# The value side of a head on the other head's partitions, in a kernel for an RG-LRU and RWKV-7 trunk

## The chip, the core and the metric

One core of one Trainium2 chip runs the whole layer as one program. The metric is the device time of one execution in microseconds; lower is better. The time before is 2658.46 us, the median of three runs (2656.79 to 2659.37).

## What is computed

One layer over 512 tokens of width 2048: a projection of the normed input, two token mixers beside each other (an RG-LRU on 1024 channels, RWKV-7 on 16 heads of 64 channels), an output projection, a gated FFN with a short causal convolution, a gated embedding and a last norm. The change touches RWKV-7. Cut to it, the reference is:

```python
def wkv7_scan(r, decay, k, v, kk, kka):
    def step(state, inp):
        r_t, w_t, k_t, v_t, kk_t, b_t = inp
        sa = jnp.einsum('bhvk,bhk->bhv', state, -kk_t)
        state = (state * w_t[:, :, None, :] + sa[..., None] * b_t[:, :, None, :]
                 + v_t[..., None] * k_t[:, :, None, :])
        y = jnp.einsum('bhvk,bhk->bhv', state, r_t)
        return state, y
...
        y = wkv7_scan(rh.astype(jnp.float32), heads(decay), kh.astype(jnp.float32),
                      vh.astype(jnp.float32), kk, kk * ah)
        mean = jnp.mean(y, axis=-1, keepdims=True)
        var = jnp.mean(jnp.square(y - mean), axis=-1, keepdims=True)
        yn = ((y - mean) * lax.rsqrt(var + LNX_EPS)).reshape(B, S, D_RWKV).astype(x.dtype)
        yn = yn * rwkv_lnx_w[i] + rwkv_lnx_b[i]
        bonus = (jnp.sum(rh * kh * rwkv_rk[i], axis=-1, keepdims=True) * vh).reshape(B, S, D_RWKV)
        out_b = (yn + bonus) * g
        h = h + jnp.concatenate([out_a, out_b], axis=-1) @ w_o[i]
```

Each head keeps a 64x64 state that is decayed, corrected and added to at every token.

## The kernel before, in words

**Dense products.** Every large product is made of three: each operand is split into a high and a low part (`split`, `wfill_`), and `dense` (lines 157, 159, 161) multiplies high by high, low by high and high by low, each a product of 128 rows, 128 columns and 512 moving columns. The weights come by DMA into `wraw`, and ScalarE and VectorE make `whi` (line 127) and `wlo` (line 128) of them.

**Phase 1** does the projection, both mixers and the first part of the output projection; **phase 2** the rest of the output projection, the FFN and what follows (lines 1170 and on). The change lies in phase 1, in the steps for the RWKV heads.

**Head pairs.** Two heads of 64 channels share a tile of 128 partitions: head half 0 on partitions 0 to 63, half 1 on 64 to 127. There are eight such pairs (`NP`). The 512 tokens are cut into eight chunks of 64 (`NC`, `C`). For each pair:

- `prep` makes, from the projections `kt`, `rt`, `vt`, the decayed operands: `bt` and `ktl` (lines 698 to 705), `AR` (709, 710), the gate `gt` and the bonus `bv`, and `pcs`, the decay of each whole chunk.
- `batch` does what needs no state, for all eight chunks. `scores` (764 to 771) multiplies `bt` and `ktl` by `AR`, chunk by chunk and half by half (64 rows, 64 columns, 128 moving columns), and VectorE masks the results into `MQ` and `NQ`. `prod` (808 to 813) makes products of 32x32 tiles, four quarters at a time, which double the size of a triangular inverse from 2 to 32; line 849 and line 862 close it to 64, `TT`. `turn` (782 to 791) transposes an operand (ScalarE copies, VectorE transposes 32x32 blocks) into `vk`, `ak`, `bk`, `kk2`. `each` (774 to 779) makes 16 products of 64 rows, 64 columns and 64 moving columns, one per chunk and half, and ScalarE copies the result out: `X1` from `NQ` and `vk`, `WT` from `ak` and `TT`, and `X1` again from `TT` and `X1`.
- `chain` (874 to 923) carries the state `st` through the chunks: `us` from `st` (lines 891, 893), the new state from `kk2` times `vk` (897) plus `bk` times `us` (906), scaled by the chunk's decay and added to the decayed old state `so` (912 to 914), and the output `y` from `vk` times `NQ` (899), `st` times `AR` (902) and `us` times `MQ` (917). All of these are 64x64x64 products, one per half.
- `norm` (926 to 943) normalizes `y`, adds the bonus and gates.

Every one of the 64-row products of before works on one half: its operands lie on the 64 partitions of that half, and so do its results. The products are full float32 (not split); in the trace each leaves two records.

**What sets the order.** On TensorE the order is that of the code (`manual_schedule`). `merge` (359 to 423) interleaves the generators: the dense stream yields after each product, and `prep`, `chain`, `batch` and `norm` yield the time on TensorE that their step is thought to take and the delay until the next step. The delays are the table `W` (line 17): `t0`, `tg`, `tt` for the batch, `lu`, `ls` for the chain, `dpace` the least distance. `duo` (732 to 747) runs the chain of one pair and the batch of the next in lockstep: a round is one step of each, back to back, followed by dense products. The chain has 15 steps, the batch 12. VectorE, ScalarE, GpSimd and SyncE are ordered by a scheduler that goes by the priorities set with `high_priority`; each engine then works strictly in that order.

**Buffers.** The results of small products go to three PSUM buffers `wk` (`aux`), two `ch` and one `y`; those of the dense stream to two `mm`.

Of the kernel before, what the change touches and what calls it, by code (L numbers as in the profile page):

```python
# [52 lines left out]
def shape_constants():  # L53
# [21 lines left out]
    c[:, o:o + 128] = (p[:, None] // 64 == p[None, :] // 64) / 64.0  # L75
# [10 lines left out]
class Builder:  # L86
# [441 lines left out]
    def lora_z(self):  # L528
# [29 lines left out]
        for tt in range(4):  # L558
            z = self.t(k1, ("vk", "bk", "kk2", "vk")[tt], (128, LW), bufs=2)
            SC.activation(z, ps[tt][:, 0:LW], AF.Copy)  # L560
            self.zl.append(z)
# [188 lines left out]
    def batch(self, j, q):  # L750
# [13 lines left out]
        def scores(src, dst, half):  # L764
            ps = wk()
            for i in range(4):
                c = 4 * half + i
                for hs in H2:
                    TE.matmul(ps[hs, i * 128:(i + 1) * 128].rearrange("p (a t) -> p a t", a=2), src[hs, c * C:(c + 1) * C],
                              AR[hs, :, c, :], start=True, stop=True)  # L770
            V.tensor_tensor(dst[:, half * 4:half * 4 + 4, :], ps.rearrange("p (i t) -> p i t", t=128), m3, ALU.mult)


        def each(lhs, rhs, dst):
            ps = wk()
            for c in range(NC):
                for hs in H2:
                    TE.matmul(ps[hs, c * C:(c + 1) * C], lhs(hs, c), rhs(hs, c), start=True, stop=True)
            SC.activation(dst, c3(ps), AF.Copy)


        def turn(n, src, bufs):
            d_ = T(n, bufs, (128, NC, C))
            SC.activation(fl(d_), src, AF.Copy)
            s3 = c3(src)
            for h in range(2):
                for i in range(2):
                    a_, b_ = 64 * h + 32 * i, 64 * h + 32 * (1 - i)
# [4 lines left out]
        for half in range(2):  # L793
            scores(bt, MQ, half)
# [21 lines left out]
        for b in (2, 4, 8, 16):  # L816
# [6 lines left out]
            if b == 2:  # L823
                scores(ktl, NQ, 0)
            with self.tc.high_priority(offset=W['offt'] - self.OFFS):
                if b == 2:

                    vk = turn("vk", vt, 2)
# [7 lines left out]
                if b == 16:  # L836
                    kk2 = turn("kk2", ktl, 2)
# [4 lines left out]
            if b == 2:  # L842
                scores(ktl, NQ, 1)
# [12 lines left out]
        X1 = NQ[:, :, 0:64]  # L856
# [733 lines left out]
```

## Time and profile before

| | |
|---|---|
| median of three runs | 2658.46 us (2656.79 to 2659.37) |
| the profiled execution | 2656.44 us, of which its span 2654.6 us |
| TensorE products busy | 2631.0 us |
| VectorE busy | 1698.6 us |
| ScalarE busy | 1089.4 us |
| stretch 70 to 850 us (the eight head pairs) | TensorE 773.90 of 780.00 us, VectorE 487.16, ScalarE 395.09 |

The span goes from the first to the last instruction of one execution; the profiled execution's own time is 1.8 us longer. In the profile PE stands for TensorE's products, PEld for its weight loads, DVE for VectorE, ACT for ScalarE, POOL for GpSimd, SP for SyncE. A row of the timeline gives the start in us, the length in us, the engine, the line, the operation, what is written and what it is made from (without buffer numbers), the shape, and how many records it merges; in brackets stands the idle time before it. Ends of products are modelled, so the distance between starts is what they cost in a stream. A row of the groups gives the count after x, then busy time, the mean length of one in ns, and idle time before with what ended it.

### The profile page before, as it was taken

The numbers are of one execution on the slowest core, as the hardware profiler recorded it, in microseconds if no ns is written. First come the engines' busy times: TensorE is split into PE (matmuls) and PEld (weight loads), VectorE is DVE, ScalarE is ACT, GpSimd is POOL, SyncE is SP. The second block draws the span as 40 slices with busy tenths as digits, with TensorE's granted clock in tenths as the row PEclk, the third lists the DMA queues.
The fourth block names the chain that finished last, engine by engine and source line by source line (L and its number), as shares of the span: only waits on it lengthen the run. The fifth ranks groups of instructions, "written<-read, shape, count | busy, mean of one in ns | idle before, by whom it ended". The sixth has DMA issues, their size and how long they took to land.

```text
span 2654.6 us, 43517 instructions
## 1 busy us (share of the span) xinstructions
PE 2631.0 (99%) x18434; PEld 2164.0 (82%) x18434; DVE 1698.6 (64%) x2356; ACT 1089.4 (41%) x1554; POOL 218.9 (8%) x177
## 2 busy tenths in 40 slices
PE   9999999999999999999999999999999999999997
PEld 8877777787777888888888888888888888888887
DVE  5764676477655635667676766766666667775447
ACT  6474546446533433333333333333333333335335
POOL 0010101001111300000000000000000000000000
PEclk9999999999999999999999999999999999999999
DMA  7222222222333322232232323233232323332223
GB/s 250 90 77 69 81 77 73 69 84 78 100 124 117 115 88 95 98 109 97 99 106 95 103 96 103 97 102 104 98 109 97 110 96 103 104 107 85 99 92 108
DMA packets 84483, 265.56 MB, mean 100 GB/s; under 512 B 9792, under 2 KB 12480, under 8 KB 84288
## 3 DMA queue, kind: packets, MB, share of 16 engines
q1 hardware_dynamic: 84288, 262.78, 30.0%
q8 instruction: 144, 2.36, 0.4%
q14 instruction: 51, 0.42, 0.1%
HBM read 254.62 MB, written 8.13 MB: 99 GB/s over the span
## 4 chain that ended last, share of the span: by engine, by line
PE 86%; DVE 3%; ACT 2%; issue 1%; POOL 1%; DMA 0%; POOLq 0%; DVEq 0%; ACTq 0%
PE wk L1212 12%; PE wk L1213 12%; PE wk L1211 12%; PE mm L1294 6%; PE mm L1295 6%; PE mm L1293 6%; PE mm L161 5%; PE mm L159 5%; PE mm L157 5%; PE mm L1384 2%; PE mm L1386 2%; PE mm L1385 2%; PE wk L812 1%; PE mm L1211 1%; PE mm L1213 1%
## 5 line engine op out<-in xcount | busy, mean ns | idle before, releaser
L127 ACT ACTIVATE whi<-wraw 128x1024 fp32r<-128x1024 f32 (+1 forms) x361 | 373.9, 1036 | 707.3 <-PE mm L159 173.5
L128 DVE TENSOR_TENSOR wlo<-wraw,whi 128x1024 fp32r<-128x1024 f32 (+1 forms) x361 | 440.7, 1221 | 210.6 <-ACT whi L127 205.6
L1211 PE MATMUL wk<-uh,whi 128*128 128x512 f32 x1408 | 547.8, 389 | 0.0
L1212 PE MATMUL wk<-ul,whi 128*128 128x512 f32 x1408 | 547.7, 389 | 0.0
L1213 PE MATMUL wk<-uh,wlo 128*128 128x512 f32 x1408 | 547.7, 389 | 0.0
L127 ACT ACTIVATE whi<-hw 128x1024 fp32r<-128x1024 f32 x154 | 163.3, 1060 | 464.6 <-PE wk L1212 418.6
L157 PE MATMUL mm<-xh,whi 128*128 128x512 f32 x832 | 329.6, 396 | 0.9 <-DVE hT L447 0.9
L161 PE MATMUL mm<-xh,wlo 128*128 128x512 f32 x832 | 330.4, 397 | 0.0
L159 PE MATMUL mm<-xl,whi 128*128 128x512 f32 x832 | 330.1, 397 | 0.0
L1211 PEld LDWEIGHTS wk<-uh,whi 128*128 128x128 f32 x1408 | 264.4, 188 | 54.8
L1213 PEld LDWEIGHTS wk<-uh,wlo 128*128 128x128 f32 x1408 | 264.3, 188 | 54.8
L1212 PEld LDWEIGHTS wk<-ul,whi 128*128 128x128 f32 x1408 | 264.4, 188 | 54.7
L128 DVE TENSOR_TENSOR wlo<-hw,whi 128x1024 fp32r<-128x1024 f32 x154 | 188.7, 1225 | 181.1 <-ACT whi L127 178.6
L1294 PE MATMUL mm<-wlo,hid 128*128 128x512 f32 x680 | 265.1, 390 | 0.0
L1295 PE MATMUL mm<-whi,hid 128*128 128x512 f32 x680 | 264.9, 390 | 0.0
L1293 PE MATMUL mm<-whi,hid 128*128 128x512 f32 x680 | 264.8, 389 | 0.0
L1239 POOL TENSOR_TENSOR tmp<-tmp,rsa 128x512 f32<-128x512 f32 x48 | 87.5, 1822 | 1360.9 <-ACT tmp L1238 1360.9
L157 PEld LDWEIGHTS mm<-xh,whi 128*128 128x128 f32 x832 | 156.3, 188 | 35.2 <-issue 2.1
L161 PEld LDWEIGHTS mm<-xh,wlo 128*128 128x128 f32 x832 | 156.2, 188 | 33.8 <-issue 1.9
L159 PEld LDWEIGHTS mm<-xl,whi 128*128 128x128 f32 x832 | 156.2, 188 | 33.7 <-issue 1.7
L1308 DVE TENSOR_TENSOR h<-h,mm 128x512 f32<-128x512 f32 x264 | 175.1, 681 | 0.6
L1293 PEld LDWEIGHTS mm<-whi,hid 128*128 128x128 f32 x680 | 127.7, 188 | 26.3
(521 smaller groups left out, 3581.7 us busy)
## 6 DMA issues: line engine op xcount, KB each, us to landing
wraw<-wgu SPq DMA_DIRECT2D x192, 512.0 KB, 3.2
hw<-wd SPq DMA_DIRECT2D x88, 512.0 KB, 3.2
wraw<-wz SPq DMA_DIRECT2D x80, 512.0 KB, 3.6
wraw<-wpg SPq DMA_DIRECT2D x31, 512.0 KB, 3.3
wraw<-wo SPq DMA_DIRECT2D x22, 512.0 KB, 3.4
wraw<-wo SPq DMA_DIRECT2D x20, 256.0 KB, 2.9
tmp<-xT SPq DMA_DIRECT2D x16, 256.0 KB, 2.7
wraw<-wd SPq DMA_DIRECT2D x8, 512.0 KB, 3.2
```

Of the source, the lines that this page charges most:

```text
L127: nc.scalar.activation(hi, raw, AF.Copy)
L128: nc.vector.tensor_tensor(lo, raw, hi.bitcast(F32), ALU.subtract)
L157: nc.tensor.matmul(ps, hi[:, k, :], xh, start=first and i == 0, stop=False)
L159: nc.tensor.matmul(ps, hi[:, k, :], xl, start=False, stop=False)
L161: nc.tensor.matmul(ps, lo[:, k, :], xh, start=False, stop=last and i == n - 1)
L1211: TE.matmul(ps, wh[:, k, :], xh, start=h + k == 0, stop=False)
L1212: TE.matmul(ps, wh[:, k, :], xl, start=False, stop=False)
L1213: TE.matmul(ps, wl[:, k, :], xh, start=False, stop=h == 1 and k == 7)
L1293: TE.matmul(ps, x[0][:, k, ts_], w[0][:, k, :], start=first and k == 0, stop=False)
L1294: TE.matmul(ps, x[0][:, k, ts_], w[1][:, k, :], start=False, stop=False)
L1295: TE.matmul(ps, x[1][:, k, ts_], w[0][:, k, :], start=False, stop=last and k == 1)
L1308: V.tensor_tensor(o, o, ps[tt], op)
```

## The change

The value channels of a head pair are stored with the two halves swapped: `prepare` swaps them in the weights of `vt`, in `mu_v`, in the gate's `rwkv_g2`, in the norm's gain and bias and in the rows of `w_o`; the constant `bdm` gets ones where the halves differ. So a value tile of half 0 lies on partitions 64 to 127. A product whose result is on the value side then takes its operands from the partitions of one half and writes to those of the other (`H2[1 - h]`, `H2[h ^ x]`), while products within the key side stay on their half as before. `scores` for `bt` (straight) and `ktl` (crossed) are made together, chunk by chunk. `each` takes several descriptions and issues their products next to each other: `X1` (crossed) with a new `Y0` (straight), `WT` (straight) with the product of `kk2` and `vk` (crossed).

The two sums that need no state leave the chunk loop: `Y0`, the part of the output from `vk` and `NQ`, is made in the batch and added to `y` at the end; the product of `kk2` and `vk`, scaled by `pcs`, is made in the batch into `kk2`, and the loop's `so` adds it to the decayed state, on VectorE instead of ScalarE. In the loop stay, per chunk, `us` and `st` times `AR`, then `bk` times `us` and `us` times `MQ`.

The batch yields once more, between the two halves of the scores (`t1`), and no longer makes scores between its 32x32 products. `vk` has one buffer instead of two. The table `W` has other numbers.

```diff
-W = dict(offw=10000, offp=[0, 300, 300, 100, 5000, 1000, 466], offl=100, offt=-100, pace=381, dpace=1914, late=16634, offs=3000, offd=300, start=1346, lora=5719, dec=0, rsk=8216, ready=23343, bonus=38816, t0=7550, tg=2186, tt=1559, lx=3928, lu=1429, ls=891, g1=1221753, g2=4936, g3=7972, per=[2, 3, 2, 2, 3, 1, 3, 0], dec7=2070)
+W = dict(offw=20000, offp=[0, 0, -100, -100, 5000, 1000, 5000], offl=0, offt=1000, pace=829, dpace=1914, late=16634, offs=45674, offd=20000, start=1496, lora=7732, dec=0, rsk=12832, ready=6791, bonus=38816, t1=891, t0=5837, tg=1544, tt=3247, lx=12605, lu=1133, ls=378, g1=2540239, g2=4936, g3=5800, per=[2, 3, 2, 3, 1, 2, 3, 0], dec7=1579)
...
-    c[:, o:o + 128] = (p[:, None] // 64 == p[None, :] // 64) / 64.0
+    c[:, o:o + 128] = (p[:, None] // 64 != p[None, :] // 64) / 64.0
...
-        def scores(src, dst, half):
-            ps = wk()
+        def scores(half):
+            pm_, pn = wk(), wk()
             for i in range(4):
                 c = 4 * half + i
-                for hs in H2:
-                    TE.matmul(ps[hs, i * 128:(i + 1) * 128].rearrange("p (a t) -> p a t", a=2), src[hs, c * C:(c + 1) * C],
-                              AR[hs, :, c, :], start=True, stop=True)
-            V.tensor_tensor(dst[:, half * 4:half * 4 + 4, :], ps.rearrange("p (i t) -> p i t", t=128), m3, ALU.mult)
+                for ps, src, x in ((pm_, bt, 0), (pn, ktl, 1)):
+                    for h in range(2):
+                        TE.matmul(ps[H2[h ^ x], i * 128:(i + 1) * 128].rearrange("p (a t) -> p a t", a=2), src[H2[h], c * C:(c + 1) * C],
+                                  AR[H2[h], :, c, :], start=True, stop=True)
+            for ps, dst in ((pm_, MQ), (pn, NQ)):
+                V.tensor_tensor(dst[:, half * 4:half * 4 + 4, :], ps.rearrange("p (i t) -> p i t", t=128), m3, ALU.mult)
-        def each(lhs, rhs, dst):
-            ps = wk()
+        def each(*what):
+            r = [c3(wk()) for _ in what]
             for c in range(NC):
-                for hs in H2:
-                    TE.matmul(ps[hs, c * C:(c + 1) * C], lhs(hs, c), rhs(hs, c), start=True, stop=True)
-            SC.activation(dst, c3(ps), AF.Copy)
+                for ps, (lhs, rhs, x) in zip(r, what):
+                    for h in range(2):
+                        TE.matmul(ps[H2[h ^ x], c, :], lhs[H2[h], c, :], rhs[H2[h], c, :], start=True, stop=True)
+            return r
...
-        for half in range(2):
-            scores(bt, MQ, half)
+        scores(0)
+        yield 960, W['t1']
+        scores(1)
...
-            if b == 2:
-                scores(ktl, NQ, 0)
...
-            if b == 2:
-                scores(ktl, NQ, 1)
...
-        each(lambda hs, c: NQ[hs, c, 0:64], lambda hs, c: vk[hs, c, :], X1)
+        for dst, ps in zip((X1, Y0), each((X1, vk, 1), (vk, Y0, 0))):
+            SC.activation(dst, ps, AF.Copy)
...
-        each(lambda hs, c: ak[hs, c, :], lambda hs, c: TT[hs, c, :], WT)
-        each(lambda hs, c: TT[hs, c, :], lambda hs, c: NQ[hs, c, 0:64], X1)
+        pw, pk = each((ak, TT, 0), (kk2, vk, 1))
+        SC.activation(WT, pw, AF.Copy)
+        V.tensor_tensor(kk2, pk, pcs.unsqueeze(2).broadcast_to([128, NC, C]), ALU.mult)
+        SC.activation(X1, each((TT, X1, 0))[0], AF.Copy)
...
             if c:
                 pu = ch()
                 for hs in H2:
                     TE.matmul(pu[hs, 0:64], MQ[hs, c, 0:64], st[hs], start=True, stop=True)
+                for h in range(2):
+                    TE.matmul(yo[H2[1 - h]], st[H2[h]], AR[H2[h], 1, c, :], start=True, stop=False)
                 us = T("us", 2, (128, 64))
                 V.tensor_tensor(us, pu[:, 0:64], NQ[:, c, 0:64], ALU.add)
-            if not last:
+                if c < NC - 1:
+                    so = T("so", 2, (128, 64))
+                    V.scalar_tensor_tensor(so, st, pc, kv[:, c, :], ALU.mult, ALU.add)
+                yield 350, W['lu']
+            if c < NC - 1:
                 ps = ch()
                 for hs in H2:
-                    TE.matmul(ps[hs, 0:64], kk2[hs, c, :], vk[hs, c, :], start=True, stop=False)
-            for hs in H2:
-                TE.matmul(yo[hs], vk[hs, c, :], NQ[hs, c, 64:128], start=True, stop=False)
...
+                    TE.matmul(ps[hs, 0:64], bk[hs, c, :], us[hs], start=True, stop=True)
+                st = T("st", 2, (128, 64))
+                V.scalar_tensor_tensor(st, ps[:, 0:64], pc, so, ALU.mult, ALU.add)
+            for h in range(2):
+                TE.matmul(yo[H2[1 - h]], us[H2[h]], MQ[H2[h], c, 64:128], start=c == 0, stop=True)
+            yield 250, W['ls']
...
-        SC.activation(sq, py, AF.Square)
-        SC.activation(y, py, AF.Copy)
+        V.tensor_tensor(y.rearrange("p (c t) -> p c t", t=C), py.rearrange("p (c t) -> p c t", t=C), NQ[:, :, 64:128], ALU.add)
+        SC.activation(sq, y, AF.Square)
...
+    def swap(a, axis=-1):
+        a = np.moveaxis(a, axis, -1)
+        return np.moveaxis(a.reshape(a.shape[:-1] + (NP, 2, 64))[..., ::-1, :].reshape(a.shape), -1, axis)
-        cols += [w[:, ZR + 1024:ZR + 2048][:, s], w[:, ZR:ZR + 1024][:, s], w[:, ZR + 2048:ZR + 3072][:, s]]
+        cols += [w[:, ZR + 1024:ZR + 2048][:, s], w[:, ZR:ZR + 1024][:, s], swap(w[:, ZR + 2048:ZR + 3072])[:, s]]
```

How the instructions move is shown at three places; x2 is one product per head half, x8 and x32 are merged likewise. The changed kernel's lines are numbered a little differently: 772 is the matmul of the scores, 822 that of `prod`, 902 and 904 are `us` and `st` times `AR`, 914 and 918 `bk` times `us` and `us` times `MQ`, 909 `so`, 916 `st`, 775 the mask.

First, TensorE in a round of a chain beside the 32x32 products of the next pair's batch, before:

```order
L161 MATMUL mm_4323<-xh_94_443,wlo_4250 128x512
L891 MATMUL ch_4498<-st_4438,MQ_3253 64x64 x2
L897 MATMUL ch_4503<-vk_3380,kk_543_3761 64x64 x2
L899 MATMUL y_4265<-NQ_3254,vk_3380 64x64 x2
L902 MATMUL y_4265<-AR_3063,st_4438 64x64 x2
L812 MATMUL wk_4510<-Tm_4299,MQ_4277 32x16 x32
L157 MATMUL mm_4323<-xh_97_461,whi_4249 128x512
```

The same kind of round on TensorE in the changed kernel:

```order
L157 MATMUL mm_5563<-xh_81_381,whi_5464 128x512
L902 MATMUL ch_5659<-st_5595,MQ_4357 64x64 x2
L904 MATMUL y_5477<-AR_4209,st_5595 64x64 x2
L822 MATMUL wk_5668<-Gm_5632,Tt_5546 32x16 x32
L159 MATMUL mm_5563<-xl_82_382,whi_5464 128x512
```

The products of `kk2` with `vk` and of `vk` with `NQ` are gone from the round, and the straight product L902 stands next to the crossed one, L904.

Second, TensorE at the start of the second head pair's batch, before:

```order
L897 MATMUL ch_2028<-vk_1306,kk_265_1638 64x64 x2
L899 MATMUL y_2027<-NQ_1186,vk_1306 64x64 x2
L906 MATMUL ch_2028<-NQ_1186,bk_1528 64x64 x2
L917 MATMUL y_2027<-MQ_1185,NQ_1186 64x64 x2
L769 MATMUL wk_2041<-AR_1870,bt_1811 64x128 x8
L769 MATMUL wk_2051<-AR_1870,bt_1811 64x128 x8
```

And now:

```order
L914 MATMUL ch_2088<-NQ_1187,bk_1537 64x64 x2
L918 MATMUL y_2087<-MQ_1186,NQ_1187 64x64 x2
L772 MATMUL wk_2097<-AR_1967,bt_1958 64x128 x2
L772 MATMUL wk_2098<-AR_1967,ktl_1963 64x128 x2
L772 MATMUL wk_2097<-AR_1967,bt_1958 64x128 x2
```

The scores from `bt` and from `ktl` alternate, chunk by chunk; before, those from `ktl` came a round later, behind the first 32x32 products.

Third, VectorE at the same head pair, where it makes `ktl`, before:

```order
L805 STREAM_TRANSPOSE Tm_2061<-Tt_2062 128x256
L703 TENSOR_TENSOR kt_1137<-kt_1137,ta_1661 128x512
L705 TENSOR_TENSOR ktl_1816<-kt_1137,th_1654 128x512
L981 TENSOR_TENSOR row_111<-mm_2005,rs_94 128x512
L893 TENSOR_TENSOR us_2129<-ch_2126,NQ_1186 128x64
```

And now:

```order
L128 TENSOR_TENSOR wlo_2076<-wraw_2073,whi_2075 128x1024
L916 SCALAR_TENSOR_TENSOR st_2091<-ch_2088,pcs,kk_268_1658 128x64
L703 TENSOR_TENSOR kt_1137<-kt_1137,ta_1684 128x512
L909 SCALAR_TENSOR_TENSOR so_2133<-st_2091,pcs,kk_268_1658 128x64
L705 TENSOR_TENSOR ktl_1963<-kt_1137,th_1677 128x512
L775 TENSOR_TENSOR MQ_2095<-wk_2097,con_175 128x512
```

`ktl` now stands behind the chain's first `st`, which reads what L914 above has made, and ahead of the first mask.

More of the change, by code (lines that the diff above doesn't have):

```diff
@@ L836, in batch @@
                 if b == 16:
-                    kk2 = turn("kk2", ktl, 2)
+                    kk2 = turn("kk2", ktl, 2, 1)
             yield 1100, W['tg']
@@ L886, in chain @@
             us = NQ[:, c, 0:64]
-            last = c == NC - 1
+            pc = pcs[:, c:c + 1]
+            so = kv[:, c, :]
             if c:
@@ L916, in chain @@
[L916 to L918 removed]
+                    TE.matmul(ps[hs, 0:64], bk[hs, c, :], us[hs], start=True, stop=True)
+                st = T("st", 2, (128, 64))
+                V.scalar_tensor_tensor(st, ps[:, 0:64], pc, so, ALU.mult, ALU.add)
+            for h in range(2):
+                TE.matmul(yo[H2[1 - h]], us[H2[h]], MQ[H2[h], c, 64:128], start=c == 0, stop=True)
+            yield 250, W['ls']
```

47 lines of the change are left out of this document (16 added, 31 removed).

## The prediction

> **What bounds the kernel now.** First the page, for which engine is full, then the busy time of the stage that the change touches.
>
> ```profile
> span 2654.6 us, 43517 instructions
> PE 2631.0 (99%) x18434; PEld 2164.0 (82%) x18434; DVE 1698.6 (64%) x2356; ACT 1089.4 (41%) x1554; POOL 218.9 (8%) x177
> PE 86%; DVE 3%; ACT 2%; issue 1%; POOL 1%; DMA 0%; POOLq 0%; DVEq 0%; ACTq 0%
> core 0: us, PE busy (x) PEld busy (x) DVE busy (x) ACT busy (x) POOL busy (x), PEclk, DMA share, GB/s
> 70.00:850.00 780.00, 773.90 (x9925) 616.01 (x9923) 487.16 (x838) 395.09 (x641) 92.22 (x79) 1.00 0.27 84
> ```
>
> TensorE (PE) is busy 99% of the span and carries 86% of the chain that ended last. In the stretch from 70 to 850 us, in which all eight head pairs run, it lacks 6.1 of 780 us; VectorE is busy 62% and ScalarE 51% of it. So time taken off PE's own stream there should come off the end, unless PE begins to wait. Its waits in that stretch are few:
>
> ```profile
> engine line waited for: us in total, times, longest us
> PE wk L769 <- DVE ktl L705: 1.6, 1, 1.6
> PE ch L891 <- DVE st L914: 0.9, 1, 0.9
> PE wk L769 <- DVE y L932: 0.8, 1, 0.8
> PE mm L157 <- DVE hT L1093: 0.8, 2, 0.6
> PE mm L1009 <- ACT lt L1016: 0.5, 1, 0.5
> PE wk L1009 <- ACT lt L1016: 0.5, 1, 0.5
> PE wk L949 <- ACT lxl L1016: 0.2, 1, 0.2
> ```
>
> They sum to 5.3 us. Now the price of the small products, from the timeline of one round (start, length, engine, line, tiles, records). A product in full float32 leaves two records, so x4 is two products: one per head half.
>
> ```profile
> 387.12 0.39 PE L161 MATMUL mm<-xh,wlo 128*128 128x512 f32 x1
> 387.44 0.33 PE L891 MATMUL ch<-st,MQ 64*64 64x64 f32 x4
> 387.55 0.20 PEld L897 LDWEIGHTS ch<-vk,kk 64*64 64x64 f32 x4
> 387.60 0.28 PE L897 MATMUL ch<-vk,kk 64*64 64x64 f32 x4
> 387.72 0.28 PE L899 MATMUL y<-NQ,vk 64*64 64x64 f32 x4
> 387.81 0.23 DVE L893 TENSOR_TENSOR us<-ch,NQ 128x64 f32<-128x64 f32 x1 [1.84 <-PE ch L891]
> 387.83 0.28 PE L902 MATMUL y<-AR,st 64*64 64x64 f32 x4
> 388.05 0.73 PE L812 MATMUL wk<-Tm,MQ 32*32 32x16 f32 x64
> 388.70 0.50 PE L157 MATMUL mm<-xh,whi 128*128 128x512 f32 x1
> 389.04 0.39 PE L159 MATMUL mm<-xl,whi 128*128 128x512 f32 x1
> ```
>
> Lengths overlap, so starts are read. L897, L899 and L902 start 0.12 and 0.11 us apart: I take 0.117 us for a pair (both halves, 64 columns), and two such pairs 0.234. Between L902 and the 32x32 products of L812 lie 0.22 us, so going from 64x64 to 32x32 tiles costs some 0.10 more than a pair. For the scores, with 128 columns:
>
> ```profile
> 457.48 0.28 PE L917 MATMUL y<-MQ,NQ 64*64 64x64 f32 x4
> 457.60 1.92 PE L769 MATMUL wk<-AR,bt 64*64 64x128 f32 x32
> 459.44 0.50 PE L161 MATMUL mm<-xh,wlo 128*128 128x512 f32 x1
> ```
>
> Eight pairs take 1.84 us with about 0.09 for leaving (as much as 387.12 to 387.44 exceeds the dense 0.23), so 0.22 us each: twice the columns, twice the time.
>
> **The change, part by part.** Per head pair, in pairs of products. Before: 16 score pairs; 24 in the three calls of `each`; in the chain 4 for chunk 0, 6 for each of chunks 1 to 6 and 4 for chunk 7, together 44. That is 68 pairs of 64 columns, 68 x 0.117 = 7.96, and 16 x 0.22 = 3.52: 11.48 us.
>
> After, products on the diagonal (rows of a half to its own columns) and across (to the other half's) stand next to each other, as the rows of the order show. Four that run side by side are a quad: 8 of scores, 8 and 8 in the first two calls of `each`, 14 in the chain; pairs remain in the third `each` (8) and at chunk 7 (1). The number of products hardly falls (the chain loses 30, `each` gains 32): everything hangs on what a quad costs.
>
> No row of before has two products on the same 64 rows and different columns, so the quad is bounded. From below by the pair, 0.117 and 0.22; from above by two pairs, 0.234 and 0.44, and more if going between the two columns costs anything. I take the lower end. The nearest row is L812: its four products stand on four different quarters and 64 records pass in 388.05 to 388.70, 0.010 us each, so PE starts products on different tiles far faster than a pair's 0.117 needs (eight records of a quad: 0.08). After: 39 x 0.117 + 8 x 0.22 = 6.32 us. Gain 5.16 us per head pair, 41.3 in all.
>
> The Trainium skill is on both sides here. "TensorEngine Tiling (Array Packing)", Key Properties, says that tiles load and multiply independently and that only a change of tiling mode drains the engine: by it a quad is a pair, and the sum stands. "TensorE: Matmul & The Clock Gate", Part 3, says that a weight load overlaps a running matmul only where its row group differs: by it a quad is two pairs and the 41.3 us shrink to nothing. The trace goes against the second as it is worded: the loads of L897 start at 387.55 while L891, on the same rows, runs until 387.77. But no run yet shows a load beside another column's product.
>
> Smaller terms. NQ's scores no longer stand behind the products of L812, so two changes from 32x32 back to 64x64 go: 2 x 8 x 0.10 = -1.6 us. The first head pair gets one round more (the new yield; in the others the chain's 15 rounds cover the batch's 13): +0.3, the 0.09 of entering, the 0.11 of leaving (388.70 to 389.04 against 0.23) and some drain. Together -1.3.
>
> The other engines' work:
>
> ```profile
> L914 DVE SCALAR_TENSOR_TENSOR st<-ch,pcs,so 128x64 f32<-128x64 f32 x48 | 13.4, 280 | 53.2 <-PE ch L906 50.4 <-ACT xh L143 2.7
> L771 DVE TENSOR_TENSOR NQ<-wk,con 128x512 f32<-128x512 f32 x16 | 10.8, 678 | 3.7 <-PE wk L769 3.6
> L705 DVE TENSOR_TENSOR ktl<-kt,th 128x512 f32<-128x512 f32 x8 | 8.3, 1035 | 0.1
> L703 DVE TENSOR_TENSOR kt<-kt,ta 128x512 f32<-128x512 f32 x8 | 5.8, 730 | 0.2 <-ACT ta L702 0.2
> L913 ACT ACTIVATE so<-st,pcs 128x64 f32<-128x64 f32 x48 | 16.6, 345 | 92.8 <-DVE st L914 88.9 <-DVE st L910 3.7
> L779 ACT ACTIVATE NQ<-wk 128x512 f32<-128x512 f32 x16 | 9.6, 598 | 3.3 <-PE wk L778 3.3
> ```
>
> VectorE gains per head pair six `so` (0.28, by L914), the product of `kk2` with `pcs` and the sum `y` (0.68 each, by L771): 3.0 us, 24 in all. ScalarE loses six `so` (0.345) and the copy of `y`, and gains the copy of Y0 and half a turn more: about -1.5 us. In a stretch of 740 us VectorE would stand at 511, 69%: its cover is PE's dense products between rounds, and I cost it at nothing by itself; without cover the 24 us would be the price. DMAs and their count stay; that the weights' order in `per` moves costs nothing while DMA is 27% busy.
>
> **New waits.** The first scores now need `ktl`, not `bt` alone. At the second head pair the order has VectorE do `ktl` behind the chain's first `st`, which itself waits for the product L914 that PE issues directly ahead of the scores. So PE stands there for: product to VectorE 0.37 (387.44 to 387.81), `st` 0.28, `kt` 0.73, `so` 0.28, `ktl` 1.04, 2.7 less some 0.4 of overlap, 2.3 us. Behind it in PE's queue stand all dense products. In the other head pairs `ktl` stands ahead of the chain's first `st`. Second, the last round of a batch fills all three `wk` buffers at once; the next user waits for a product of 0.68 and copies of 0.60: nothing if five dense products lie between, up to 1.2 us for each of 8 pairs. Third, PE gives back some 43 us that covered the same chain of steps; the waits of 5.3 us may as well double. Bounds: 2 and 22 us more; I take 12, near 2.3 + 5 + 5.
>
> **The sum.** The profiled execution took 2656.4 us (span 2654.6). 2656.4 - 41.3 - 1.3 + 12 = 2625.8. The median of the runs is 2.0 above the profiled one, so 2628. With waits of 2 to 22 it is 2618 to 2638.
>
> **Rivals.** First, weights are loaded one tile after the other within the same 64 rows, while the products run together. A load of 64 columns keeps the pair's pace (L897's loads take the 0.117 step), so a 64-column quad would cost 0.234, and the score quad, 0.22, would hide both loads. Then only the scores gain: 8 x 8 x 0.22 = -14.1, 64-column work 69 pairs for 68, +0.9, -1.3, and waits of 8: 2656.4 - 6.5 + 2.0 = 2652. For it: the pair's pace shows loads and products equally long. Against it: L812's four loads do not queue, though those are on four row groups.
>
> Second, and this is how the change would not do what it says: the same 64 rows take one product at a time. (It is what the second page named above would make of it.) Quads are two pairs: +0.9 - 1.3 + 3 of waits, 2659 + 2 = 2661, no change. The planner's table, made for shorter rounds, would then be merely out of step.
>
> Third, slower: a move between the two column halves drains PE as a change of tile size does, 0.10 us into and out of the second pair. 38 quads x 8 = 304, in turn and with 0.20 each: +61, 2656.4 + 61 + 2.0 + 2 = 2721. It decides from a price of about 0.10 us per quad above the pair (30.6 us of gain over 304), so from 0.22 for 64 columns. Against it: no drain shows between L891, L897, L899 and L902, though these never change columns.
>
> **How the numbers follow.** Forecast 0.71: the row of L812 and the overlap of loads speak for it, and no row denies it. First rival 0.12, second 0.10, third 0.07. Range: from 2616, just below the forecast with the fewest waits, to 2655, which takes in the first rival with 3 us to spare; that leaves some 0.2 outside. A measurement of this kernel can tell 0.2%, 5.3 us, from no change. Faster by more: forecast and nearly all of the first rival, 0.82. Within: the second and a little of the first, 0.11. Slower: 0.07.
>
> **What would show it.** In the profile after, in the timeline of a round: chunk 1's two kinds of products, now 8 records, should pass in about 0.12 us before the next line starts; 0.23 says the second rival, or the first if the 32 records of scores(0) still take 0.9 instead of 1.8. More than 0.25 says the third. In the waits of PE, a row for `ktl` of 2 to 3 us at one place, and waits in the 70 to 850 us stretch of 8 to 27 in total. The forecast is wrong if the stretch with the head pairs is not at least 20 us shorter, or if PE's busy share falls below 97% there.

## The result and the profile after

The changed kernel takes 2645.03 us (median of 4 runs, 2643.15 to 2646.38) where the kernel before took 2658.49 on the same chip (2656.79 to 2659.37): a ratio of 0.995, 95% interval 0.9932 to 0.9967. It is faster, by 13.5 us; 30.5 had been forecast. The page, and the stretch of the head pairs from 70 to 850 us:

```profile
span 2641.3 us, 43552 instructions
PE 2599.0 (98%) x18466; PEld 2131.1 (81%) x18466; DVE 1720.5 (65%) x2420; ACT 1082.4 (41%) x1515; POOL 218.3 (8%) x177
70.00:850.00 780.00, 755.12 (x10012) 594.38 (x10011) 519.55 (x914) 394.65 (x612) 94.65 (x81) 0.99 0.28 88
```

TensorE's busy time fell by 32.0 us (2631.0 to 2599.0), the span by 13.3 only: the part of the span in which TensorE is idle grew from 23.6 to 42.3 us, 18.7 more. In the stretch it is now idle for 24.9 us instead of 6.1. Two questions follow: why 32 and not 42 us less work, and where the 18.7 us of waiting come from.

First the products, in the timeline (start, length, engine, line, tiles, records). A round of the chain, the same one as before, and the dense product ahead of it:

```profile
387.97 0.39 PE L157 MATMUL mm<-xh,whi 128*128 128x512 f32 x1
388.29 0.27 PE L902 MATMUL ch<-st,MQ 64*64 64x64 f32 x2
388.30 0.27 PE L904 MATMUL y<-AR,st 64*64 64x64 f32 x2
388.40 0.23 PE L902 MATMUL ch<-st,MQ 64*64 64x64 f32 x2
388.41 0.22 PE L904 MATMUL y<-AR,st 64*64 64x64 f32 x2
388.56 0.73 PE L822 MATMUL wk<-Gm,Tt 32*32 32x16 f32 x64
```

The four products on the four quarters start within 0.01 us (388.29 and 388.30), their second passes 0.11 us later, and the next size begins 0.27 us after the first start. Before, each pair took 0.12 us for itself here. The scores of half a head pair:

```profile
373.96 0.28 PE L772 MATMUL wk<-AR,bt 64*64 64x128 f32 x2
373.98 0.28 PE L772 MATMUL wk<-AR,ktl 64*64 64x128 f32 x2
374.07 0.28 PE L772 MATMUL wk<-AR,bt 64*64 64x128 f32 x2
...
374.74 0.28 PE L772 MATMUL wk<-AR,ktl 64*64 64x128 f32 x2
374.95 0.50 PE L159 MATMUL mm<-xl,whi 128*128 128x512 f32 x1
```

Eight products of each kind, four quads, pass from 373.96 on, 0.11 us for each pass and two passes for a quad (373.96, 374.07): 0.22 us, as long as one kind alone took before. So the quad costs what the pair cost. Summed over all groups of 64x64 products (from the first record of a group to the record behind it, the median of the groups that hold no wait, times their number), these products and the steps into other sizes take 112.6 us before and 71.0 after: 41.6 us less.

Now the waits of TensorE (engine, what it waits for, who releases it: total us, times, longest):

```profile
PE wk L772 <- DVE ktl L705: 8.1, 3, 5.2
PE y L918 <- DVE us L906: 2.9, 3, 1.6
PE wk L1010 <- ACT Gm L858: 2.6, 1, 2.6
PE wk L822 <- DVE Tm L815: 2.4, 1, 2.4
PE wk L772 <- DVE MQ L775: 2.1, 3, 1.3
PE mm L1010 <- DVE row L1000: 1.9, 1, 1.9
PE wk L256 <- DVE y L253: 1.5, 1, 1.5
PE wk L713 <- ACT MQ L876: 1.4, 1, 1.4
```

The rows of Gm L858, MQ L775 and MQ L876 are waits for a `wk` buffer that such a step still reads, those of `ktl`, `us` and Tm waits for data. They are few and single: nine among the head pairs, of over 1.2 us each, make up 19.2 of the 26.6 us of all rows, most of them where one head pair gives way to the next (150 to 190, 289 to 291, 464 to 473, 609 to 650 us). And they cost twice. Each line of the next view is a stretch of 3.41 us, with TensorE's busy time in it, its records, the clock that it was granted there, and the DMA's share and rate; the last two rows are stretches with waits behind which the clock stays whole:

```profile
151.62:155.03 3.41, 1.55 (x7) 1.00 0.50 159
155.03:158.44 3.41, 3.41 (x39) 0.50 0.00 0
185.76:189.17 3.41, 0.00 (x0) 1.00 0.50 154
189.17:192.58 3.41, 3.30 (x31) 0.50 0.02 5
469.06:472.47 3.41, 1.69 (x23) 1.00 0.27 67
472.47:475.88 3.41, 3.41 (x32) 0.50 0.21 87
609.01:612.42 3.41, 1.55 (x9) 1.00 0.00 0
612.42:615.83 3.41, 2.86 (x7) 0.50 0.02 5
646.56:649.97 3.41, 1.21 (x66) 1.00 0.40 124
649.97:653.38 3.41, 3.41 (x16) 0.50 0.77 260
182.34:185.76 3.42, 1.74 (x18) 1.00 0.54 206
288.15:291.56 3.41, 1.93 (x30) 1.00 0.69 231
```

After each of the five stretches in which TensorE is busy for less than half (1.55, 0.00, 1.69, 1.55, 1.21 us of 3.41) it gets half the clock for one stretch. The kernel before has none among its head pairs (granted clock 1.00 from 70 to 850 us). In the five half-clock stretches TensorE is busy for 16.4 us. Dense products start every 0.43 us in them and every 0.23 us elsewhere, so the whole clock would do this work in about half the time: an estimate of 8.2 us lost. The account closes to 1.4 us: -41.6 for the products, +8.2 for the clock, +18.7 for the idle time, together -14.7, and the span shows -13.3.

### The profile page after: what moved, and what is told of

Its sections match the earlier page's. It is cut to its first block, busy times and chain, and to the rows that moved or that the text cites. A ratio compares the mean times of both kernels' runs of the same rounds, so it can differ in the third digit from the quotient of the medians.

```text
span 2641.3 us, 43552 instructions
## 1 busy us (share of the span) xinstructions
PE 2599.0 (98%) x18466; PEld 2131.1 (81%) x18466; DVE 1720.5 (65%) x2420; ACT 1082.4 (41%) x1515; POOL 218.3 (8%) x177
## 4 chain that ended last, share of the span: by engine, by line
PE 69%; DVE 2%; ACT 1%; issue 1%; DMA 0%; POOL 0%; DVEq 0%; POOLq 0%; ACTq 0%
PE wk L1212 12%; PE wk L1213 12%; PE wk L1214 12%; PE mm L1295 6%; PE mm L1294 6%; PE mm L1296 6%; PE mm L1385 2%; PE mm L1386 2%; PE mm L1387 2%; PE mm L157 2%; PE mm L161 2%; PE mm L159 2%; PE mm L1212 1%; PE mm L1214 1%; PE mm L1213 1%
## 5 line engine op out<-in xcount | busy, mean ns | idle before, releaser
L128 DVE TENSOR_TENSOR wlo<-wraw,whi 128x1024 fp32r<-128x1024 f32 (+1 forms) x361 | 440.5, 1220 | 208.0 <-ACT whi L127 202.2
L128 DVE TENSOR_TENSOR wlo<-hw,whi 128x1024 fp32r<-128x1024 f32 x154 | 188.7, 1225 | 181.6 <-ACT whi L127 179.1
```

The lines of the kernel that those rows point to most:

```text
L128: nc.vector.tensor_tensor(lo, raw, hi.bitcast(F32), ALU.subtract)
```

## The experiments

Theory 1, after this reading: the price of the quad was right, and the 28 us given back are waits at single places and the half clock behind them, because rounds now stand closer on TensorE than the steps of VectorE and ScalarE between them last. The rivals are stated with each run. In the table, idle is the span less TensorE's busy time, both from the page of the profiled run, and the last column counts stretches of 3.41 us at half clock among the head pairs. The ratio is to the kernel before on the same chip and is what compares runs best, since that kernel varies from 2656.5 to 2658.5 us.

| run | median us | ratio (95% interval) | PE busy | idle | half clock |
|---|---|---|---|---|---|
| before | 2658.49 | 1 | 2631.0 | 23.6 | 0 |
| after | 2645.03 | 0.995 (0.9932 to 0.9967) | 2599.0 | 42.3 | 5 |
| e1_apart | 2649.41 | 0.997 (0.9958 to 0.9982) | 2613.7 | 34.7 | 5 |
| e2_old_table | 2656.77 | 0.9997 (0.9988 to 1.0006) | 2608.5 | 47.3 | 11 |
| e3_table_alone | 2670.34 | 1.0052 (1.0035 to 1.0068) | 2634.4 | 33.6 | 3 |
| e4_ktl_first | 2645.44 | 0.9957 (0.9942 to 0.9972) | 2599.9 | 43.4 | 6 |
| e5_filler | 2680.25 | 1.0084 (1.0067 to 1.0101) | 2637.9 | 41.7 | 8 |
| e6_dve_light | 2647.75 | 0.9961 (0.9946 to 0.9976) | 2602.2 | 44.3 | 7 |
| e7_warm | 2644.84 | 0.995 (0.9935 to 0.9965) | 2607.9 | 36.8 | 5 |
| e8_retuned | 2632.07 | 0.9903 (0.9889 to 0.9918) | 2596.4 | 36.8 | 4 |
| e9_dense_fill | 2669.66 | 1.0044 (1.0027 to 1.0061) | 2630.4 | 37.3 | 8 |
| e10_wk4 | 2641.92 | 0.9941 (0.9925 to 0.9958) | 2596.9 | 42.4 | 4 |
| e11_filler_behind | 2667.71 | 1.004 (1.0026 to 1.0054) | 2629.6 | 35.1 | 3 |
| e12_wk4_retuned | 2630.02 | 0.99 (0.9883 to 0.9916) | 2594.1 | 34.8 | 4 |

**e1: the two kinds one after the other.**

```
-            for i in range(4):
-                c = 4 * half + i
-                for ps, src, x in ((pm_, bt, 0), (pn, ktl, 1)):
+            for ps, src, x in ((pm_, bt, 0), (pn, ktl, 1)):
+                for i in range(4):
+                    c = 4 * half + i
...
-            for c in range(NC):
-                for ps, (lhs, rhs, x) in zip(r, what):
+            for ps, (lhs, rhs, x) in zip(r, what):
+                for c in range(NC):
```

> The changed kernel, but in the scores and in the calls of `each` all products on the diagonal are issued first and all products across after them, so that nothing but the chain's products stands side by side. Theory 1 (the price of the quad was right, the waits were undersized): per head pair 8 score quads become two pairs each, 8 x 0.22, and 16 quads of `each` become two pairs, 16 x 0.117: 3.6 us, 29 us in all, of which the longer rounds give some 3 to 8 us back by covering waits: 2666 to 2671 us, and TensorE's waits fall below the 26.6 us of the changed kernel. Rival (the quads saved little and that is why the gain is small): at most 10 us slower, 2655 us or less.

The time is the rival's (2649.41, where it said 2655 or less), but not for the rival's reason, since the quad's price was read above as forecast. The profiled span is 7.1 us longer than after the change, the ratio 0.997 for 0.995, with intervals that overlap. TensorE's busy time rose by 14.7 us, not 29, and its idle time fell by 7.6. The rows of one call of `each` show why it rose so little:

```profile
237.86 0.97 PE L783 MATMUL wk<-vk,NQ 64*64 64x64 f32 x26
238.62 0.27 PE L783 MATMUL wk<-NQ,vk 64*64 64x64 f32 x2
238.67 0.28 PE L783 MATMUL wk<-vk,NQ 64*64 64x64 f32 x3
...
238.79 0.92 PE L783 MATMUL wk<-NQ,vk 64*64 64x64 f32 x25
```

In this call the kind across comes first (26 records). The first products of the second kind, on the diagonal, start at 238.62, while six records of the first are still to come: TensorE takes them ahead of the program's order, on the free quarters. The call (64 records, from its first to its last start, the median of the eight) takes 1.69 us, side by side 0.94; two calls of 32 in a row took 1.82 before. So side by side is worth 0.75 us in such a call, and half of the work that was given back here, 7.6 of 14.7 us, took the place of waits.

**e2 and e3: code and table, each alone.** e2 is the change with the line `W` of before (and `t1=891`), e3 the kernel before with the line `W` of the change.

> The changed kernel with the planner's table of before (its one new entry t1 kept). Theory 1 (waits come from rounds that the plan places too close for VectorE and ScalarE, and the new table was fitted to that): with the old table the waits of TensorE grow from 26.6 to some 35 to 45 us, with more half-clock stretches: 2652 to 2665 us. Rival (the new table is what brings the waits, the code is fine): waits fall to 10 to 15 us, 2628 to 2633 us.

> The kernel before with the new table of numbers alone. Theory 1 (the table is fitted to the new code, and hardly matters to the old): 2658 to 2666 us, waits of TensorE 8 to 14 us. Rival (the new table brings the waits by itself): the waits rise from 8.0 to 20 us or more, with half-clock stretches, 2668 us or more.

With the table of before the new code is as fast as the old code (0.9997): 47.3 us idle, eleven half-clock stretches. Theory 1 has the time of e2, though not its waits: idle time rose by 5 us only (the waits sum to 31 us, below the 35 to 45 expected), and the half clock did the rest. With the new table the old code is slower by 13 us (1.0052), 10.0 us of it idle time, with three stretches, so in e3 it is the rival's time that came, with waits of 18 us, a little below its 20: the table brings waits by itself. Both hold together only if a table is fitted to one code. Neither part of the change is worth anything alone; together they give 13.5 us.

**e4: `ktl` ahead of the chain.**

```
-        SC.activation(ta, ta, AF.Identity, scale=self.dv("kah", j), bias=self.dv("kac", j))
...
+        with self.tc.high_priority(offset=60000):
+            SC.activation(ta, ta, AF.Identity, scale=self.dv("kah", j), bias=self.dv("kac", j))
...
```

> The changed kernel with the four steps that make kt and ktl raised above the chain's steps, so that VectorE never does a step of the chain ahead of ktl. Theory of the prediction (the scores wait since ktl stands behind st): the 8.1 us of waits for ktl go, and with them the half-clock stretches at 189 and 472 us, some 1.5 us each: 2633 to 2636 us. Rival (the whole chain of steps around the start of a round of head pairs is late, and ktl is only what comes last): the wait moves to the chain's own steps, at the second head pair to a product that waits for X1 or st, 3 to 5 us there: 2642 to 2646 us.

The rival's number. The 5.2 us at the second head pair did not go, they have another name (lines here are one higher):

```profile
PE ch L915 <- ACT NQ L879: 4.6, 1, 4.6
PE y L919 <- DVE us L907: 3.2, 3, 1.6
```

The chain's first product now waits for the copy of X1, which ScalarE begins at 188.25 us only, behind copies for the transposes and a weight split. The round as a whole stands too early there; `ktl` was only what came last.

**e5 and e11: TensorE's time given back.** Both are e1 with three useless pairs in seven rounds of each chain; with them TensorE's busy time is within 7 us of that before. In e5 they write into the tile that `us` is made from, in e11 behind the round's last product.

```
+                for _ in range(3):
+                    for hs in H2:
+                        TE.matmul(pu[hs, 64:128], bk[hs, c, :], bk[hs, c, :], start=True, stop=True)
```

> The kernel of e1_apart (scores and `each` with the products across behind those on the diagonal) with, in addition, three useless pairs of 64x64 products in each chain round that makes `us`, behind the products that are needed, into columns that nobody reads: TensorE's small work is then back near that of before (17 us from e1, 7 x 8 x 0.34 = 19 us from the filler, against a gain of 41.6), while order, table and VectorE's work stay those of the change. Theory 1 (the waits come up because TensorE's work no longer covers the steps of the other engines): waits fall from the 26.6 us of the changed kernel to 10 to 18 us, and the half-clock stretches to one or two: 2656 to 2666 us. Rival (the waits belong to the new order and to VectorE's added work, whatever TensorE does): waits stay at 25 us or so, and the 36 us are paid in full: 2679 to 2683 us.

> As e5_filler, but the three useless pairs stand behind the last product of each chain round that makes `st`, and write to columns of y that are written anew in the next round, so that no step of another engine waits for them (in e5 they wrote to the tile that `us` is made from, and `us` started 0.94 us after the round's first product instead of 0.62). TensorE's small work is again 17 + 19 us above the change. Theory 1 (the waits come up because the rounds became shorter than the steps between them): waits of 10 to 16 us as against 26.6, two half-clock stretches or fewer: 2658 to 2667 us, so that some 15 to 22 of the 36 us are free. Rival (e5 stands: the waits stay whatever TensorE does): 25 us of waits, 2676 to 2683 us.

e5 fits the rival, but it is a poor test: `us` had to wait for the filler, so it lengthened the steps as well as TensorE's work. In e11 nothing waits for it, and the answer is between the two: 35.1 us idle, three stretches, 10 us slower than before. Against e1 the filler is paid in full (span +16.3, busy +15.9 us). And the first scores wait as long as ever:

```profile
PE wk L772 <- DVE ktl L705: 7.6, 3, 6.3
```

So theory 1 is right in part only. Giving TensorE nearly all its work back takes 7.2 us of the 18.7 of idle time away, all of it in the scores and in `each`; the other 11 or so came with the new order and table, and e3's 10.0 us for the table alone is close to that. Such sums are rough, since each edit moves steps on VectorE too.

**e9: work added elsewhere.** The first product of each dense group of the first phase three times over.

```
+                for _ in range(2 if first and i == 0 and self.MM == 2 else 0):
+                    nc.tensor.matmul(ps, hi[:, k, :], xh, start=True, stop=True)
```

> The changed kernel with the first product of each dense group of the first phase done three times instead of once (the two extra ones are overwritten): 128 useless dense products, 29 us, spread evenly over the stream, not in the rounds. Theory A (TensorE's lost work leaves too little cover in general): waits fall from 26.6 us to 16 or less, with two half-clock stretches or fewer: 2655 to 2662 us. Theory B (a wait comes where one round stands too close behind the steps that it needs, and work elsewhere in the stream doesn't help): waits of 20 us or more, and nearly all of the 29 us is paid: 2667 to 2676 us.

Theory B: 21 us of waits, idle time 37.3 us, and 24.6 of the 29 us paid (2669.66 for 2645.03). Work elsewhere in the stream shortens the waits by some 5 of 26 us, with three half-clock stretches more; that what stands directly ahead of a wait decides is the reading, not a thing this run shows by itself.

**e6: VectorE's added work.** This kernel leaves out the decayed state that is carried from chunk to chunk, the scaling by `pcs` and the sum with `Y0`, so it computes something else.

```
-        V.tensor_tensor(kk2, pk, pcs.unsqueeze(2).broadcast_to([128, NC, C]), ALU.mult)
+        SC.activation(kk2, pk, AF.Copy)
...
-                    V.scalar_tensor_tensor(so, st, pc, kv[:, c, :], ALU.mult, ALU.add)
...
-        V.tensor_tensor(y.rearrange("p (c t) -> p c t", t=C), py.rearrange("p (c t) -> p c t", t=C), NQ[:, :, 64:128], ALU.add)
+        SC.activation(y, py, AF.Copy)
```

> The changed kernel with VectorE's three added kinds of steps taken off it: the decayed state plus kv is left out (st is made from kv alone, so the state isn't carried on), the product of kv with pcs becomes a copy on ScalarE, and the sum of y with Y0 a copy on ScalarE. VectorE has 26.7 us less to do, ScalarE 9.6 more. Theory of the prediction (TensorE's products cover VectorE's added work, cost nothing): 2642 to 2649 us, with waits of 22 to 30 us, some of them at other places. Rival (it is the added work on VectorE that makes TensorE wait): waits fall below 15 us: 2628 to 2634 us.

Nothing gained (0.9961 for 0.995), idle time 44.3 us: the added work on VectorE is not what TensorE waits for. This step of the prediction stands.

**e7: useless work inside two waits.**

```
+            for _ in range(20 if j == 1 and half == 0 else 0):
+                TE.matmul(pm_, self.wx[:, 0:128], self.xs[0][0], start=True, stop=True)
...
+            for _ in range(9 if j == 6 and vk is None else 0):
+                TE.matmul(ps, self.wx[:, 0:128], self.xs[0][0], start=True, stop=True)
```

> The changed kernel with useless dense products inside two of its longest waits: 20 ahead of the first scores of the second head pair (4.5 us into a wait of 5.2) and 9 ahead of the first 32x32 products of the seventh (2.0 us into a wait of 2.4). TensorE gets 6.5 us more work. Theory (the half-clock stretches of 3.41 us are the price of standing still, paid on top of each long wait): the stretches that start at 189 and 650 us are gone, three are left, the waits for ktl and Tm shrink to 0.7 and 0.4 us: 2640 to 2643 us, faster by 1.5 to 3 us in spite of more work. Rival (the half clock comes for another reason, or costs nothing because the waits are long enough anyway): 2645 us or, where the useless work delays what it stands ahead of, up to 2651 us.

The stretch at 189 us is gone and idle time is 5.5 us lower, so 6.5 us of work cost nothing. But the half clock now comes at 338 us, and behind another wait at 656 instead of 650, and the time is that of the change, 2644.84 us where the theory said 2640 to 2643. What the half clock costs by itself is therefore read from the trace (8.2 us), not shown by this run.

**e8, e10 and e12: better placing.** e8 changes ten numbers of the table. e10 gives `wk` a fourth buffer and `ch` one less. e12 has both, with twelve numbers.

```
-... offp=[0, 0, -100, -100, 5000, 1000, 5000], ... pace=829, ... offd=20000, ... lora=7732, ... t1=891, ... lx=12605, lu=1133, ... g2=4936, g3=5800, ... dec7=1579)
+... offp=[0, 0, -100, 3000, 5000, 1000, 5000], ... pace=790, ... offd=300, ... lora=6934, ... t1=488, ... lx=19227, lu=467, ... g2=4106, g3=5782, ... dec7=1286)
```

> The changed kernel with other numbers in the planner's table (ten entries, among them the pause t1 between the two halves of the scores 488 for 891, lora 6934 for 7732, offd 300 for 20000, the priority of the stage that makes ktl 3000 for -100), and not a line of code changed. Theory 1 (the 28 us that were given back are a matter of where the plan puts the rounds, not of the quads): some of the waits go, from 26.6 us to 12 to 20, with one to three half-clock stretches: 2630 to 2640 us. Rival (the waits lie in the length of the dependent steps themselves, and no placing helps): 2643 to 2652 us.

> The changed kernel with four `wk` buffers in PSUM instead of three; the bank comes from `ch`, which has one buffer instead of two (since the change each product into `ch` waits anyway for the step that reads the one before; at the start of the program four `wk` buffers take the place of two and two). Theory of the prediction (part of the new waits is the want of a `wk` buffer when two calls take two each): the waits for Gm, MQ and the copy at L876, 2.6, 2.1 and 1.4 us, go, and with the first of them the half-clock stretch at 155 us: 2637 to 2641 us. Rival (what waits for a buffer would wait for data a little later): those rows go, but rows for ktl, us, Tm or the lower-rank gates grow by as much: 2643 to 2648 us.

> e10's four `wk` buffers and e8's kind of table together (twelve entries differ from the change's table, no other line of code). Theory (the fourth buffer takes waits away once the rounds stand right, and the table does most): waits and half-clock stretches below those of e8, that is TensorE's idle time below 36.8 us and at most three stretches: 2626 to 2632 us. Rival (the two remedies cure the same waits): no better than e8, 2632 to 2637 us.

e8 is 13 us faster than the change without a line of code, 0.9903 against 0.995, and the intervals do not meet. The trace explains a part of it: its execution, the slowest of the four, has a span 8.1 us shorter than that of the change, 5.5 of it idle time and 2.6 busy time, with one half-clock stretch less. No row for `ktl` is left among its waits; the longest are:

```profile
PE wk L822 <- DVE Tm L815: 4.4, 3, 1.7
PE ch L902 <- DVE st L916: 3.0, 3, 2.3
PE wk L772 <- DVE MQ L775: 2.6, 3, 1.3
```

In e10 the waits for Gm and MQ are down to 0.3 and 0.2 us, and the half-clock stretch at 155 us is gone, as the prediction's term would have it. But the product at L713, which waited 1.4 us for the copy at L876, still waits for a `wk` buffer, now the one that VectorE reads at L877 (`kk2` is none of its operands), and the idle time is the same (42.4 us): other waits took their place, as the rival says.

```profile
PE wk L772 <- DVE ktl L705: 6.9, 3, 3.9
PE wk L822 <- DVE Tm L815: 4.3, 2, 2.9
PE y L918 <- DVE us L906: 3.6, 3, 2.3
...
PE wk L713 <- DVE kk L877: 1.7, 1, 1.7
```

Its time, 2641.92 us, lies between the two expectations, and 0.9941 is not told apart from 0.995. e12, at 0.99, beats both kernels but not measurably e8. Its idle time and its time are the theory's (34.8 and 2630.02 us), its four half-clock stretches are one too many. Whether the fourth buffer adds anything to a table that fits is not shown.

## Why the prediction was right, and where it went wrong

**The price of the quad** held. 0.117 and 0.22 us were taken, and the trace shows the same periods; 41.3 + 1.3 us were forecast for products and changes of size, 41.6 came. The sign that the prediction set for it was badly put: 0.27 us pass in the round above from the quad's first start to the next line, more than the 0.25 that was to speak for the third rival, because the step into 32x32 tiles is in it. Before, the four pairs of such a round took 0.61 us to the same point (387.44 to 388.05): three pairs less make 0.34, where 0.35 was to be expected. The choice of the lower end, by the 32x32 products on four quarters, was right, and with it the rule of "TensorEngine Tiling (Array Packing)", Key Properties, in the Trainium skill, that tiles of one mode work independently. The rule of "TensorE: Matmul & The Clock Gate", Part 3, in the Trainium skill, would have given 2661 us; the timeline shows four products on two sets of rows starting within 0.01 us. The first and third rival fell with the same rows.

**VectorE's 24 us at nothing** held: VectorE's busy time rose by 21.9 us, and e6 shows that taking the work away gains nothing, though it puts 8 us on ScalarE instead.

**The wait for `ktl`** was at the place that was named, but 5.2 us long instead of 2.3. VectorE there, in the changed kernel, and GpSimd beside it:

```profile
184.45 1.23 DVE L128 TENSOR_TENSOR wlo<-wraw,whi 128x1024 fp32r<-128x1024 f32 x1 [0.99 <-ACT whi L127]
185.59 0.28 DVE L916 SCALAR_TENSOR_TENSOR st<-ch,pcs,kk 128x64 f32<-128x64 f32 x1
185.78 1.56 DVE L703 TENSOR_TENSOR kt<-kt,ta 128x512 f32<-128x512 f32 x1
187.26 0.27 DVE L909 SCALAR_TENSOR_TENSOR so<-st,pcs,kk 128x64 f32<-128x64 f32 x1
187.46 1.77 DVE L705 TENSOR_TENSOR ktl<-kt,th 128x512 f32<-128x512 f32 x1
185.01 1.78 POOL L1037 TENSOR_TENSOR rsa<-rsa,lrc 128x512 f32<-128x512 f32 x1 [8.18 <-ACT rsa L1034]
187.42 1.26 POOL L718 TENSOR_TENSOR rt<-rt,kt 128x512 f32<-128x512 f32 x1 [0.62 <-DVE kt L703]
```

The prediction counted from `st` on. Ahead of `st` stood a weight split (the L128 of the order rows that went with it), which itself waited for ScalarE and ended at 185.68: 1.7 us more. And `kt` and `ktl` took 1.56 and 1.77 us, not the means of 0.73 and 1.04, since each began while GpSimd was at a step on tiles of that size: they end at 187.34 and 189.23, each 0.55 us behind the end of GpSimd's step (186.79 and 188.68). The Trainium skill says why, in "SBUF — State Buffer", SBUF: two separate sides: VectorE, in a step with two inputs in SBUF, and GpSimd share a pair of ports as a lock, and whichever starts first keeps it for the whole instruction. The trace agrees in the main: both steps of VectorE end behind GpSimd's, though 0.55 us behind, where such a step takes 0.69 alone. These sizes, 1.7, 0.83 and 0.73 us, make the 2.9 between with a little overlap. It also said that `ktl` stands ahead of the chain elsewhere; two more waits for it came, 1.5 us each. And e4 shows that the mechanism was told too narrowly: with `ktl` out of the way, the round waits for X1.

**The `wk` buffers** (5 us) were sized about right as rows: Gm 2.6, MQ 2.1, the copy 1.4, together 6.1. But e10 shows that they are not a cost of their own: the size was met by luck.

**The old waits** were to double from 5.3, and did: of 24.7 us in the rows of the stretch, 8.1 are `ktl` and 6.1 `wk`, 10.5 the rest. With these the waits in the rows grew by 19.4 us where 12 was taken, still inside the bounds of 2 and 22.

**What was missing** is the half clock: 8.2 us, no term of the sum and no bound. The trace of before could not show it, since none of its waits among the head pairs is long enough. The Trainium skill has it, in "TensorE: Matmul & The Clock Gate", HAM oscillation: a gap beyond some 3.4 us sends the clock to half. By that rule only the wait of 5.2 us would have; among the head pairs of this trace it came after each stretch of which half (1.7 us) or more was idle.

So the failed step is the term for new waits, +12 us. It came out at some 28, the 41.6 us less the 13.3 that the span shows: 19 of waiting, 8 of half clock, the rest not accounted for. Both tests that the prediction set itself say so: the part with the head pairs is 11 to 13 and not 20 us shorter (the last chain's last product ends at 818.6 for 829.8 us, VectorE's last L447 behind it at 836.8 for 850.3), and TensorE's busy share there is 96.8%, below 97. Behind the size stands a reading that was left out: the prediction took the new table for a detail ("merely out of step"), while e2, e3 and e8 show that the numbers which place the rounds are worth as much as the whole gain, 12 to 14 us each way.

What stays open: which share of the 19 us each cause has. The sizes above come from different edits, each of which moves other steps too, and the half clock's 8 us are read from the trace alone. Open too is how much of the idle time this code needs with the best table. e12 still has 11 us more of it than before, and which of its waits another order would take away was not tried. No run gives `vk` its second buffer back; in the trace no step that writes `vk` waits for TensorE.

## What to carry to other kernels

When the engine that sets the time gets less work, take its saving from the timeline, but ask of each place where its program waits in order what now stands ahead of that place and how long the other engines' steps between take there; read those steps at the place itself, not as means over the kernel. A hand-set plan is part of a change: run new code with the old numbers and old code with the new ones, and refit before judging. Where a wait empties half of a clock stretch, expect a second price behind it; here it was up to 1.7 us each time.

## What the runs showed of the hardware

- Among the head pairs of the changed kernel the clock falls to half for 3.41 us after each stretch of 3.41 us in which TensorE was busy for less than half, on a fixed grid: the five drops begin at 155.03, 189.17, 472.47, 612.42 and 649.97 us, 10, 83, 41 and 11 times 3.413 us apart. Busy times of 1.69 and 1.74 us lie on the two sides. The other traces show that the records' busy time isn't exactly the measure: in e5 a stretch with 1.62 us (from 182.14) is followed by the whole clock, and drops follow stretches with 2.73 us (e7, at 338.22), 2.71 (e9, at 345.15), 2.82 (e8, at 332.55) and 3.09 (e2, at 595.38). In each of these four, about 1 us of the records are products of 2 columns. Half clock can also last longer, 6.83 us in e10 (from 187.49) and 10.24 in e1 (from 186.71).
- TensorE starts products of one size on free quarters past others that stand ahead of them in the program: in e1 six records ahead, in a call of 64 records that took 0.12 us less than two calls of 32 in a row did before (1.69 for 1.82).
- In the changed kernel a product of two tiles of 128x512 elements on VectorE (`kt`, `ktl`) that begins during a GpSimd step of that size ends 0.55 us after it, and takes 1.4 to 1.8 us. Where VectorE begins first it keeps its 0.69 us (`ktl` at 103.5 and 290.4 us) and GpSimd's step takes 1.7 to 1.8 us instead of 1.26. In the kernel before, too, `ktl` took 1.64 us at 187.9 us, which its mean of 1.04 hid.
